# A transformer block on one core: silu, sums of squares and a third of the first modulation columns moved to TensorE's row and column groups

## The chip, the cores and the metric

One core of a Trainium2 chip runs the whole program. The metric is device microseconds of one execution; before the change the median of three runs is 1647.77 us (1646.96 to 1654.14).

## The reference, cut to what matters

The block has 256 tokens of width 2048. What matters here is its beginning:

```python
mod = silu(c) @ w_ada + b_ada                 # c: 2048, w_ada: 2048 x 12288
sh1, sc1, gt1, sh2, sc2, gt2 = split(mod, 6)
h = rms_norm(x, norm1_g) * (1.0 + sc1) + sh1  # x: 256 x 2048
proj = h @ w_in                               # w_in: 2048 x 10064
```

Behind it come a recurrent mix (RWKV-7), a sparse attention, a merge, an output projection and a feed-forward part of width 8192. All is fp32 to the outside; the change touches nothing behind proj.

## The kernel before, in words

x and h stand transposed, 16 chunks of 128 model columns by 256 tokens. Each weight is split on the chip into a high part, rounded by ScalarE (`whi`, line 193), and a low part, the difference, by VectorE (`wlo`, line 90); h likewise (`hhi`, `hlo`). A product is three matmuls (`mm3`): high by high, high by low, low by high.

**The modulation.** Column e of mod (128 values) is a dot product of 128 rows of w_ada transposed with silu(c), which stands on every partition (`sb`). `ada_long` (line 164) loads one such tile of 128x2048 (1 MB) into a slot of `ap0` or `ap1` on the SP queue, and VectorE multiplies and sums it in one operation (line 158), which gives one column of `modc`. Four slots are used for the first four loads, afterwards two (`SLOTS`).

**silu(c).** c arrives as one row of 2048; four fp32 matmuls with a row of ones spread it over the partitions (`cps`), ScalarE takes a tanh, VectorE forms twice the silu in `sb`.

**The squares.** ScalarE squares x in eight pieces of two chunks, VectorE adds them up (`sqs`, seven additions), and two matmuls with ones sum over the partitions (`pss`); `rsqrt` makes the factor `rs` of it.

**The rounds.** h is needed chunk by chunk, and chunk j needs columns j (shift) and 16 + j (scale). So the first projections run in five rounds over chunks 0-1, 2-3, 4-7, 8-11 and 12-15 (`rounds`). In each round `modulate` (line 325) forms am, hf, hhi and hlo of its chunks; then nine groups of columns of w_in are multiplied with them: one of 352 columns, eight of 512. `proj` (line 244) takes a group; for each pair of chunks it loads a weight tile (`weights`, 512 KB, four `raw` buffers, three each of whi and wlo) and lets `next_ada` load columns of the next round at an even pace (`pace`). From the second round on VectorE adds a group's PSUM to what stands in SBUF; the two groups of v stay in PSUM. Of two pairs a group has two weight tiles, so the second round has 9 tiles and the third and fourth 18.

The order of the work is set by priorities (`prio`: START first, then STREAM for weights, MAIN for matmuls) and a scheduler that simulates a timeline and writes each engine's instructions in one fixed order. Each engine, and the SP queue that issues these loads, then works strictly in that order.

Of the kernel before, what the change touches and what calls it, by code (L numbers as in the profile page):

```python
# [11 lines left out]
FT = mybir.dt.float32  # L12
# [5 lines left out]
T = 256  # L18
# [5 lines left out]


P_BADA, P_N1, P_N2, P_MU, P_A0, P_KK, P_KA, P_RK, P_LNW, P_LNB = 0, 96, 112, 128, 155, 163, 171, 179, 187, 195
P_QG, P_KG0, P_KG1, P_KG2, P_PEK, P_PEV, NPRM = 203, 204, 205, 206, 207, 223, 239

C_ID, C_MSK, C_HS, C_ONE, C_BLK, C_CUM, C_SEL, NCST = 0, 128, 192, 224, 225, 353, 609, 737

# [2 lines left out]
def block_kernel(ctx, tc, a):  # L33
# [32 lines left out]
    def B8(name, shape, dt=FT):  # L66
        return b8.tile(shape, dt, name=name, tag="b8")
# [4 lines left out]
    def T2(name, shape, dt=FT):  # L72
        return t2.tile(shape, dt, name=name, tag="t2")
# [7 lines left out]
    def PM(name, shape=(128, 512)):  # L81
        return pmm.tile(list(shape), FT, name=name, tag="pm")
# [3 lines left out]
    def act(out, in_, func, **kw):  # L86
        return S.activation(out, in_, func, **kw).ins  # L87

    def tt(out, x, y, op):
        return V.tensor_tensor(out, x, y, op=op).ins  # L90
# [7 lines left out]
    def mm(out, l, r, start=True, stop=True):  # L98
        return PE.matmul(out, l, r, start=start, stop=stop, skip_group_check=True).ins  # L99
# [10 lines left out]

    tc.cur_priority = START
    sb = sbp.tile([128, D], FT, name="sb", tag="sb")
    crow = B8("crow", [1, D])
    nc.sync.dma_start(crow, a["c"])
    one1 = cst.tile([1, 128], FT, name="one1")
    V.memset(one1, 1.0)
    xn = B16("xn", [128, KC, T])
    xT = a["xT"].rearrange("(k p) t -> p k t", p=128)
# [21 lines left out]
    ts(qg8, prm[:, P_QG:P_QG + 1], 0.125, None, OP.mult, OP.bypass)  # L140


    for i in range(4):
        ps = PM("cps")
        mm(ps, one1, crow[:, i * 512:i * 512 + 512])
        o = sb[:, i * 512:i * 512 + 512]
        lastt = act(o, ps, AF.Tanh, scale=0.5)
        stt(o, o, 1.0, ps, OP.add, OP.mult)
# [11 lines left out]

    apb = [B16("ap0", [128, 2, D]), B16("ap1", [128, 2, D])]
    apn = [0]
    SLOTS = 2

    def ada_long(e):

        n = apn[0] if apn[0] < 4 else apn[0] % SLOTS
        r = apb[n // 2][:, n % 2]
        apn[0] += 1
        nc.sync.dma_start(r, a["w_ada_t"][e * 128:(e + 1) * 128])  # L170
        ada_dot(r, sb, prm[:, P_BADA + e:P_BADA + e + 1], modc[:, e:e + 1])

    def ada(e):

        part = sm.tile([128, 1], FT, name="adap", tag="sm1")
        for h in range(2):
            r = RAW("ar", [128, 1024])
            nc.sync.dma_start(r, a["w_ada_t"][e * 128:(e + 1) * 128, h * 1024:(h + 1) * 1024])
            ada_dot(r, sb[:, h * 1024:(h + 1) * 1024], part if h else prm[:, P_BADA + e:P_BADA + e + 1],
                    modc[:, e:e + 1] if h else part)  # L180

    rounds = [(0, 2), (2, 2), (4, 4), (8, 4), (12, 4)]
    for j in range(rounds[0][1]):
# [52 lines left out]
    def next_ada(f=ada):  # L236
        pace[1] += pace[0]
        while later and pace[1] >= 1:
            pace[1] -= 1
            with prio(STREAM):  # L240
                f(later.pop(0))

    def proj(segs_of, W, ms, rhi, rlo, kps, evac, banks=None, first=True, last=True):


        nb = (len(ms) + 1) // 2
        ps = banks or [PM("pp") for _ in range(nb)]
        for i, kp in enumerate(kps):
            hi, lo = weights(segs_of(kp), W)
            next_ada(ada_long if starting[0] else ada)  # L250
            todo = [[(k, m) for m in range(len(ms))] for k in range(2)]
            if 0 and i == len(kps) - 1 and nb == 2:
                todo = [[(k, m) for k in range(2) for m in range(len(ms)) if m // 2 == b] for b in range(2)]
            for part in todo:
                for k, m in part:
                    (c0, cw), kc = ms[m], 2 * kp + k
                    o = ps[m // 2][0:cw, (m % 2) * 256:(m % 2) * 256 + 256]
                    mm3(o, hi[:, k, c0:c0 + cw], lo[:, k, c0:c0 + cw], rhi[:, kc], rlo[:, kc],
                        first and i == 0 and k == 0 and m % 2 == 0, last and i == len(kps) - 1 and k == 1)
                yield  # L260
        if evac:
            with prio(STREAM):
                for b in range(nb):
                    evac(b, ps[b])
# [17 lines left out]


    pss = PX("pss", (128, 256))
    sqs = T2("sqs", [128, 2, T])
    act(sqs, xn[:, 0:2], AF.Square)
    for i in range(1, 8):
        sq = T2("sq", [128, 2, T])
        act(sq, xn[:, 2 * i:2 * i + 2], AF.Square)
        tt(sqs, sqs, sq, OP.add)  # L290
    for k in range(2):
        mm(pss, ones, sqs[:, k], k == 0, k == 1)

    def log_exp(behind):

# [5 lines left out]
    def rsqrt(out, x, scale, ep, tmp):  # L301

        e0 = {0.0: 0, 1e-6: 1, 64e-5: 2}[ep]
        act(out, x, AF.Ln, scale=scale, bias=eps[0:x.shape[0], e0:e0 + 1])
        i = act(out, out, AF.Exp, scale=-0.5)
        tt(tmp, out, out, OP.mult)
        stt(tmp, x, ep / scale, tmp, OP.add, OP.mult)
        stt(tmp, tmp, -0.5 * scale, out, OP.mult, OP.mult)
        stt(out, out, 1.5, tmp, OP.mult, OP.add)
        return i  # L310

    rs = T2("rs", [128, T])
    with tc.issue_after(log_exp([lastt])):
        rsqrt(rs, pss, 1.0 / D, 1e-6, T2("rst", [128, T]))

    hhi = B16("hhi", [128, KC, T], FR)
    hlo = B16("hlo", [128, KC, T], FR)
# [8 lines left out]
    def modulate(j0, n, src):  # L326

        last = [None]
        for j in range(j0, j0 + n, 2):
            hf = T2("hf", [128, 2, T])  # L330
            for i in range(2):
                affine(hf[:, i], src[:, j + i], am[:, j + i:j + i + 1], rs, modc[:, j + i:j + i + 1], hhi[:, j + i], hlo[:, j + i], last)
        return last[0]

# [49 lines left out]
    for r, (j0, n) in enumerate(rounds):  # L384
        first, last = r == 0, r == len(rounds) - 1
        with prio(START + (1 << 18)):
            stt(am[:, j0:j0 + n], modc[:, 16 + j0:16 + j0 + n], 1.0, prm[:, P_N1 + j0:P_N1 + j0 + n], OP.add, OP.mult)
            lasth = modulate(j0, n, xn)
            if first:
                hold.extend([lasth] * 0 + [None])  # L390
        if not last:
            later.extend(e for j in range(j0 + n, sum(rounds[r + 1])) for e in (j, 16 + j))
            pace[:] = [len(later) / (len(groups) * n // 2 - 1), 0]
        for cols, W, ms, dst, banks in groups:
            g = proj(wseg(cols), W, ms, hhi, hlo, range(j0 // 2, (j0 + n) // 2),
                     dst and acc_evac(dst, first, last), banks, first or banks is None, last or banks is None)
            if last and dst and cols[0][0] >= 3360 and W == 512:
                queue.append(g)
            else:
                run(g)  # L400
        assert not later
    starting[0] = False
    pace[:] = [0.36, 0]

# [728 lines left out]
            lastss[0] = mm(ps[:, 0:T], ones, x[:, i], k == 0 and i == 0, k == 1 and i == 1)  # L1133
    rs2 = T2("rs2", [128, T])
    with tc.issue_after(le):
        i = rsqrt(rs2, ps[:, 0:T], 1.0 / D, 1e-6, T2("rst2", [128, T]))
    ahold[:0] = [i, i]
    for q, t in ((0, 0), (0, 1), (1, 0)):
        tokens(q, t)
# [113 lines left out]
def _pack(inp):  # L1253

    g = {k: v[0] if k != "rel_bias" else v for k, v in inp.items()}
    p = np.zeros((128, NPRM), np.float32)

    def cols(at, v):
        v = v.reshape(-1, 128)
        p[:, at:at + v.shape[0]] = v.T  # L1260

    cols(P_BADA, g["b_ada"])
    cols(P_N1, g["norm1_g"])
    cols(P_N2, g["norm2_g"])
    cols(P_MU, g["rwkv_mu"][:3328])
    p[64:96, P_MU + 26] = g["rwkv_mu"][3328:]
    for at, k in ((P_A0, "rwkv_a0"), (P_KK, "rwkv_k_k"), (P_KA, "rwkv_k_a"), (P_LNW, "rwkv_ln_w"), (P_LNB, "rwkv_ln_b")):
        cols(at, g[k])
    cols(P_RK, g["rwkv_r_k"].reshape(-1))
    for at, v in ((P_QG, g["q_norm_g"]), (P_KG0, g["k_norm_g"][0]), (P_KG1, g["k_norm_g"][1]), (P_KG2, g["k_norm_g"][2])):  # L1270
        p[:, at] = np.concatenate([v, v])
    for at, k in ((P_PEK, "cmp_pe_k"), (P_PEV, "cmp_pe_v")):
        p[:, at:at + 16] = g[k].reshape(16, 2, 64).transpose(1, 2, 0).reshape(128, 16)
    c, onehot = _consts()
    out = {
        "xT": g["x"].T, "c": g["c"], "w_ada_t": g["w_ada"].T, "w_in": g["w_in"], "params": p, "consts": c,
        "onehot": onehot, "w2a": np.concatenate([g["rwkv_w2"], g["rwkv_w0"][None]]), "a2": g["rwkv_a2"],
        "g2": g["rwkv_g2"], "w1k": g["cmp_w1_k"], "w2k": g["cmp_w2_k"], "w1v": g["cmp_w1_v"], "w2v": g["cmp_w2_v"],
        "rel_bias": g["rel_bias"], "w_o_rwkv": g["w_o_rwkv"], "w_o_nsa": g["w_o_nsa"], "w_out": g["w_out"],
        "w_up": g["w_up"], "w_down": g["w_down"],  # L1280
    }
    return {k: np.ascontiguousarray(v) for k, v in out.items()}
# [17 lines left out]
```

## Time and profile before

| | |
|---|---|
| runs: median, lowest, highest | 1647.77, 1646.96, 1654.14 us |
| profiled execution: its time | 1648.3 us |
| its span, first to last instruction | 1646.5 us |
| mean granted TensorE clock | 0.983 |
| TensorE, VectorE, ScalarE busy | 95%, 70%, 46% |

The profile is of one execution. Its busy figures are means over stages that differ much, so a stage is read by its own windows. Engine names are PE (TensorE matmul), PEld (its weight loads), DVE (VectorE), ACT (ScalarE), SPq (the queue that issues loads). Ends of matmuls are modelled, so a matmul is shown longer than the distance to the next one.

### The profile page before, as it was taken

How to read it: one execution, taken by the hardware profiler on the slowest of the kernel's cores; microseconds unless marked ns; L12 is line 12 of the kernel's file. 1: busy time of each engine (PE TensorE's matmuls, PEld its weight loads, DVE VectorE, ACT ScalarE, POOL GpSimd, SP SyncE). 2: the span in 40 equal slices, each digit the busy share in tenths (PEclk: the TensorE clock that was granted, in tenths of full speed). 3: DMA queues.
4: the chain of work that ended last, by engine and by line, in shares of the span. 5: the costliest groups of instructions: out<-in, count | busy, mean ns of one | idle time of the engine just before them, and what ended most of it. 6: DMA issues, size and time to landing. Idle time of an engine off the chain costs nothing.

```text
span 1646.5 us, 28130 instructions
## 1 busy us (share of the span) xinstructions
PE 1564.2 (95%) x11291; PEld 1380.2 (84%) x11291; DVE 1149.4 (70%) x1695; ACT 756.3 (46%) x1112; POOL 34.9 (2%) x60
## 2 busy tenths in 40 slices
PE   5969999999999889999999899999999999999998
PEld 4968998878889879777899788888888888888886
DVE  7999876977788766777876776666655555555555
ACT  4423358526423365656534444444444544444442
POOL 0000000000000000000000000000000000000001
PEclk9989999998999999999999999999999999999999
DMA  9999767673988777655687477878776555555564
GB/s 371 319 325 342 247 183 236 215 200 120 324 245 276 251 262 258 237 180 167 212 287 269 153 242 239 264 244 260 242 217 189 204 194 193 192 192 194 194 194 148
DMA packets 171174, 381.99 MB, mean 232 GB/s; under 512 B 29249, under 2 KB 43905, under 8 KB 166690
## 3 DMA queue, kind: packets, MB, share of 16 engines
q1 hardware_dynamic: 149344, 355.79, 65.6%
q0 software_dynamic: 4176, 14.17, 2.4%
q10 hardware_dynamic: 17523, 10.24, 2.2%
q8 instruction: 88, 1.44, 0.3%
q14 instruction: 43, 0.35, 0.1%
HBM read 370.13 MB, written 10.01 MB: 231 GB/s over the span
## 4 chain that ended last, share of the span: by engine, by line
PE 48%; DMA 4%; DVE 3%; issue 1%; ACT 1%; DVEq 0%; ACTq 0%
PE pu L99 21%; PE da L99 10%; PE db L99 10%; PE pp L99 5%; DMA ar<-in_w_ada_t 2%; DMA wr<-in_w_out 1%; DVE wlo L90 1%; PE po L99 1%; PE sps L99 1%; DMA gate<-sma 0%; ACT whi L193 0%; PE ptp L1012 0%; DVE ar L158 0%; DVE o L90 0%; ACT p L87 0%
## 5 line engine op out<-in xcount | busy, mean ns | idle before, releaser
L193 ACT CAST whi<-wr 128x1024 fp32r<-128x1024 f32 (+1 forms) x352 | 367.0, 1043 | 513.4 <-PE pp L99 125.6
L90 DVE TENSOR_TENSOR wlo<-wr,whi 128x1024 fp32r<-128x1024 f32 (+1 forms) x352 | 425.8, 1213 | 171.8 <-ACT whi L193 168.7
L99 PE MATMUL pp<-hhi,whi 128*128 128x256 f32 (+1 forms) x1072 | 309.9, 293 | 25.1 <-ACT hhi L87 22.5
L99 PE MATMUL pp<-hlo,whi 128*128 128x256 f32 (+1 forms) x1072 | 307.4, 289 | 0.2 <-DVE hlo L93 0.2
L99 PE MATMUL pp<-hhi,wlo 128*128 128x256 f32 (+1 forms) x1072 | 301.2, 290 | 6.6 <-DVE wlo L90 6.6
L90 DVE TENSOR_TENSOR wdl<-wd,wdh 128x1024 fp32r<-128x1024 f32 x128 | 156.6, 1225 | 170.9 <-ACT wdh L193 170.9
L99 PEld LDWEIGHTS pp<-hhi,whi 128*128 128x128 f32 (+1 forms) x1072 | 209.9, 197 | 33.8 <-ACT hhi L87 23.4
L193 ACT CAST wdh<-wd 128x1024 fp32r<-128x1024 f32 x128 | 134.9, 1055 | 193.7 <-PE db L99 188.6
L99 PEld LDWEIGHTS pp<-hhi,wlo 128*128 128x128 f32 (+1 forms) x1072 | 205.5, 196 | 13.0 <-DVE wlo L90 8.5
L99 PEld LDWEIGHTS pp<-hlo,whi 128*128 128x128 f32 (+1 forms) x1072 | 210.5, 196 | 5.0 <-issue 3.7
L99 PE MATMUL pu<-h2a,whi 128*128 128x512 f32 x512 | 177.2, 398 | 3.1 <-DVE h2a L93 3.1
L99 PE MATMUL pu<-h2b,whi 128*128 128x512 f32 x512 | 179.1, 397 | 0.8 <-DVE h2b L93 0.8
L99 PE MATMUL pu<-h2b,wlo 128*128 128x256 f32 x512 | 140.9, 280 | 0.0
L99 PE MATMUL pu<-h2a,wlo 128*128 128x256 f32 x512 | 135.9, 281 | 0.0
L158 DVE CUSTOM_DVE_ANT_0 ar<-ar,sb,prm 128x1024 f32<-128x1024 f32 x64 | 82.1, 1282 | 73.0 <-DMA ar<-in_w_ada_t 72.9
L99 PEld LDWEIGHTS pu<-h2b,whi 128*128 128x128 f32 x512 | 95.8, 188 | 23.9 <-DVE h2b L93 1.2
L99 PEld LDWEIGHTS pu<-h2a,whi 128*128 128x128 f32 x512 | 95.2, 189 | 24.4 <-DVE h2a L93 3.4
L99 PEld LDWEIGHTS pu<-h2a,wlo 128*128 128x128 f32 x512 | 95.5, 190 | 2.2
L158 DVE CUSTOM_DVE_ANT_0 ar<-ar,sb,adap 128x1024 f32<-128x1024 f32 x64 | 82.0, 1281 | 21.2 <-DMA ar<-in_w_ada_t 20.9
L99 PEld LDWEIGHTS pu<-h2b,wlo 128*128 128x128 f32 x512 | 95.9, 189 | 0.5
L99 PE MATMUL db<-wdh,ul 128*128 128x512 f32 x256 | 79.6, 389 | 0.0
L99 PE MATMUL db<-wdl,uh 128*128 128x512 f32 x256 | 79.6, 389 | 0.0
(342 smaller groups left out, 2676.6 us busy)
## 6 DMA issues: line engine op xcount, KB each, us to landing
wr<-in_w_in SPq DMA_DIRECT2D x136, 512.0 KB, 5.1
ar<-in_w_ada_t SPq DMA_DIRECT2D x128, 512.0 KB, 4.8
wr<-in_w_up SPq DMA_DIRECT2D x128, 512.0 KB, 4.3
wd<-in_w_down SPq DMA_DIRECT2D x128, 512.0 KB, 4.3
ap<-in_w_ada_t SPq DMA_DIRECT2D x32, 1024.0 KB, 6.6
wr<-in_w_out SPq DMA_DIRECT2D x32, 512.0 KB, 5.4
wr<-in_w_in SPq DMA_DIRECT2D x40, 256.0 KB, 3.4
wr<-in_w_o_rwkv SPq DMA_DIRECT2D x16, 512.0 KB, 4.9
```

The lines of the kernel that those rows point to most:

```text
L90: return V.tensor_tensor(out, x, y, op=op).ins
L99: return PE.matmul(out, l, r, start=start, stop=stop, skip_group_check=True).ins
L158: V.tensor_tensor_reduce(out=r, in0=r, in1=s, scale=0.5, scalar=start, op0=OP.mult, op1=OP.add, accum_out=out)
L193: S.copy(hi, raw)
```

## The change

Five edits:

1. c is loaded as four rows of 512 on partitions 0, 32, 64 and 96, and the four spreading matmuls take one row each, into four PSUM banks, ahead of the tanhs.
2. The squares of x go to TensorE: each piece's two halves are summed over the partitions into one of four column groups of `ps4` (16 matmuls of 32 columns), copied, and one matmul with ones sums the groups. The additions on VectorE go.
3. In the first round h is formed one chunk at a time, in later ones two.
4. `ada_long` always uses four slots.
5. For the third, fourth and fifth rounds half of the eight modulation columns come from TensorE. Of the four chunks the first two keep their four dot products. The columns of the other two are loaded as four tiles of a repacked array `w_ada_p`, 128x2048 each (`ada_rows`). Once all four are loaded, and at least three weight tiles after the last was issued, `rows_done` issues 16 fp32 matmuls with silu(c) as a weight of 32 columns, one of them not zero (`scz`), into four column groups of one PSUM bank; ScalarE copies the bank; four matmuls of one column turn the sums into four columns; two small VectorE operations add the bias. The pace is set so that the last load comes earlier in the round.

```diff
 P_QG, ..., NPRM = 203, 204, 205, 206, 207, 223, 239
...
-    crow = B8("crow", [1, D])
-    nc.sync.dma_start(crow, a["c"])
-    one1 = cst.tile([1, 128], FT, name="one1")
+    crow = T2("crow", [128, 512])
+    nc.sync.dma_start(crow.rearrange("(g r) n -> g r n", g=4)[:, 0], a["c"].rearrange("(g n) -> g n", g=4))
+    one1 = cst.tile([128, 128], FT, name="one1")
...
+    cps = [PM("cps") for _ in range(4)]
     for i in range(4):
-        ps = PM("cps")
-        mm(ps, one1, crow[:, i * 512:i * 512 + 512])
+        mm(cps[i], one1[32 * i:32 * i + 1], crow[32 * i:32 * i + 1])
+    for i, ps in enumerate(cps):
         o = sb[:, i * 512:i * 512 + 512]
...
-        n = apn[0] if apn[0] < 4 else apn[0] % SLOTS
+        n = apn[0] % 4
...
+    scz = T2("scz", [128, 16, 32])
+    V.memset(scz, 0.0)
+    sct = T2("sct", [128, 16])
+    act(sct, prm[:, P_C:P_C + 16], AF.Tanh, scale=0.5)
+    stt(scz[:, :, 0], sct, 1.0, prm[:, P_C:P_C + 16], OP.add, OP.mult)
+    loaded = []
+
+    def ada_rows(x):
+        j, q = x
+        r = apb[apn[0] % 4 // 2][:, apn[0] % 2]
+        apn[0] += 1
+        nc.sync.dma_start(r, a["w_ada_p"][(j - 6 + q) * 128:(j - 5 + q) * 128])
+        loaded.append([j, r, 0])
+
+    def rows_done(all_of_them=False):
+
+        for x in loaded:
+            x[2] += 1
+        if len(loaded) < 4 or loaded[-1][2] < 3 and not all_of_them:
+            return
+        ps = PM("adp")
+        for q in range(4):
+            for i in range(4):
+                mm(ps[32 * i:32 * i + 32], scz[:, 4 * q + i], loaded[q][1][:, i * 512:i * 512 + 512], q == 0, q == 3)
+        j = loaded[0][0]
+        del loaded[:4]
+        row = T2("adr", [128, 512])
+        S.copy(row, ps)
+        for i in range(4):
+            mm(ps[:, i:i + 1], row[:, i * 128:i * 128 + 128], one, i == 0, i == 3)
+        for i, e in enumerate((j, 16 + j)):
+            stt(modc[:, e:e + 2], ps[:, 2 * i:2 * i + 2], 0.5, prm[:, P_BADA + e:P_BADA + e + 2], OP.mult, OP.add)
...
-            next_ada(ada_long if starting[0] else ada)
+            next_ada((ada_rows if later and isinstance(later[0], tuple) else ada_long) if starting[0] else ada)
...
+                if starting[0] and part is todo[1]:
+                    rows_done()
                 yield
...
-    sqs = T2("sqs", [128, 2, T])
-    act(sqs, xn[:, 0:2], AF.Square)
-    for i in range(1, 8):
+    ps4 = PX("ps4", (128, 256))
+    for i in range(8):
         sq = T2("sq", [128, 2, T])
         act(sq, xn[:, 2 * i:2 * i + 2], AF.Square)
-        tt(sqs, sqs, sq, OP.add)
-    for k in range(2):
-        mm(pss, ones, sqs[:, k], k == 0, k == 1)
+        for k in range(2):
+            g = 2 * (i % 2) + k
+            mm(ps4[32 * g:32 * g + 32], ones[:, 0:32], sq[:, k], i < 2, i > 5)
+    sq4 = T2("sq4", [128, T])
+    S.copy(sq4, ps4)
+    mm(pss, ones, sq4)
...
-            stt(am[:, j0:j0 + n], modc[:, 16 + j0:16 + j0 + n], 1.0, prm[:, P_N1 + j0:P_N1 + j0 + n], OP.add, OP.mult)
-            lasth = modulate(j0, n, xn)
+            step = 1 if first else 2
+            for j in range(j0, j0 + n, step):
+                stt(am[:, j:j + step], modc[:, 16 + j:16 + j + step], 1.0, prm[:, P_N1 + j:P_N1 + j + step], OP.add, OP.mult)
+                lasth = modulate(j, step, xn)
...
             pace[:] = [len(later) / (len(groups) * n // 2 - 1), 0]
+            if r:
+                j = j0 + n
+
+                later[:] = [j, 16 + j, j + 1, 17 + j] + [(j + 2, q) for q in range(4)]
+                pace[:] = [8 / (len(groups) * n // 2 - 4), 0]
...
         assert not later
+        rows_done(True)
     starting[0] = False
```

Left out are small parts: c as 16 more columns of the parameters (`P_C`), the factor 32 that the row of ones of `ps4` brings into `rsqrt`'s scale, a return value of `rsqrt`, and the packing of `w_ada_p` outside the device program.

## Rows read from the trace of the kernel before

**Rows 1.** The page: its span, TensorE's total, TensorE in 40 slices.

```profile
span 1646.5 us, 28130 instructions
...
PE 1564.2 (95%) x11291; PEld 1380.2 (84%) x11291; DVE 1149.4 (70%) x1695; ACT 756.3 (46%) x1112; POOL 34.9 (2%) x60
...
PE   5969999999999889999999899999999999999998
```

**Rows 2.** Ten-us windows: busy time of each engine (x instructions), PEclk, DMA share, GB/s.

```profile
0.00:10.00 10.00, 7.05 (x8) 2.49 (x8) 4.90 (x17) 6.11 (x11) 0.20 (x4) 1.00 0.82 283
10.00:20.00 10.00, 2.19 (x5) 1.18 (x4) 9.12 (x11) 4.39 (x8) 0.00 (x0) 1.00 1.00 418
20.00:30.00 10.00, 1.94 (x7) 1.65 (x8) 9.97 (x17) 3.78 (x5) 0.00 (x0) 1.00 1.05 411
30.00:40.00 10.00, 10.00 (x76) 10.00 (x75) 6.75 (x7) 5.41 (x9) 0.00 (x0) 1.00 1.03 389
...
70.00:80.00 10.00, 10.00 (x86) 10.00 (x85) 10.00 (x10) 2.89 (x3) 0.00 (x0) 1.00 0.98 333
```

**Rows 3.** Windows, TensorE alone: busy time (x matmuls), PEclk, DMA share, GB/s.

```profile
83.00:95.20 12.20, 0.00 (x0) 0.67 0.94 326
95.20:103.00 7.80, 7.63 (x43) 0.64 0.73 262
108.00:163.00 55.00, 50.26 (x400) 0.97 0.97 345
163.00:208.00 45.00, 45.00 (x378) 1.00 0.76 251
```

**Rows 4.** TensorE's waits, 80 to 110 us and 140 to 160 us.

```profile
PE pp L99 <- ACT hhi L87: 13.4, 1, 13.4
...
PE pp L99 <- DVE wlo L90: 3.7, 3, 2.2
```

**Rows 5.** VectorE's timeline: last dot of round two, x scaled behind it.

```profile
91.70 2.35 DVE L158 CUSTOM_DVE_ANT_0 ap<-ap,sb,prm 128x2048 f32<-128x2048 f32 x1 [1.33 <-DMA ap<-in_w_ada_t]
...
94.29 1.67 DVE L93 SCALAR_TENSOR_TENSOR hf<-xn,am,rs 128x256 f32<-128x256 f32 x4
```

**Rows 6.** VectorE's groups, 95 to 206 us: low parts, dot products.

```profile
L90 DVE TENSOR_TENSOR wlo<-wr,whi 128x1024 fp32r<-128x1024 f32 (+1 forms) x35 | 40.8, 1181 | 6.8 <-ACT whi L193 6.8
L158 DVE CUSTOM_DVE_ANT_0 ap<-ap,sb,prm 128x2048 f32<-128x2048 f32 x16 | 37.5, 2345 | 3.0 <-DMA ap<-in_w_ada_t 3.0
```

**Rows 7.** Loads to 260 us: count, KB each, median us to landing.

```profile
wr<-in_w_in SPq DMA_DIRECT2D x68, 512.0 KB, 5.5
ap<-in_w_ada_t SPq DMA_DIRECT2D x32, 1024.0 KB, 6.6
```

**Rows 8.** The SP queue's own waits to 260 us: us, times, longest.

```profile
SPq L170 <- DVE modc L158: 57.2, 24, 5.3
```

**Rows 9.** TensorE's timeline: fp32 matmuls of 32 columns by 512.

```profile
281.41 0.28 PE L99 MATMUL pp<-hlo,whi 128*128 128x256 f32 x1
281.62 1.04 PE L99 MATMUL kss<-ksq,cs 128*32 128x512 f32 x2
...
288.02 1.05 PE L99 MATMUL kss<-ksq,cs 128*32 128x512 f32 x4
```

**Rows 10.** TensorE's timeline: fp32 transposes with 128x128 weights, two places.

```profile
379.81 0.60 PE L638 MATMUL vps<-cs,pv 128*128 128x128 f32 x4
380.17 0.36 PE L99 MATMUL pp<-hhi,whi 128*128 128x256 f32 x1
...
398.28 1.97 PE L660 MATMUL bkp<-cs,BK 128*128 128x128 f32 x8
```

**Rows 11.** ScalarE's groups, 28 to 206 us: the copies of a PSUM bank.

```profile
L359 ACT COPY prk<-pp 128x512 f32<-128x512 f32 x8 | 4.6, 589 | 3.6 <-PE pp L99 3.6
```

**Rows 12.** ScalarE's timeline at the start: first weight's cast, first h.

```profile
21.20 0.78 ACT L193 CAST whi<-wr 128x704 fp32r<-128x704 f32 x1 [1.44 <-DMA wr<-in_w_in]
...
27.33 0.91 ACT L87 ACTIVATE hhi<-hf,modc 128x256 fp32r<-128x256 f32 x2 [2.56 <-DVE hf L93]
```

**Rows 13.** VectorE's groups to 28 us: the additions of squares.

```profile
L90 DVE TENSOR_TENSOR sqs<-sqs,sq 128x512 f32<-128x512 f32 x7 | 4.8, 690 | 1.4 <-ACT sq L87 1.1
```

More of the change, by code (lines that the diff above doesn't have):

```diff
@@ L26 @@
 P_BADA, P_N1, P_N2, P_MU, P_A0, P_KK, P_KA, P_RK, P_LNW, P_LNB = 0, 96, 112, 128, 155, 163, 171, 179, 187, 195
-P_QG, P_KG0, P_KG1, P_KG2, P_PEK, P_PEV, NPRM = 203, 204, 205, 206, 207, 223, 239
+P_QG, P_KG0, P_KG1, P_KG2, P_PEK, P_PEV, P_C, NPRM = 203, 204, 205, 206, 207, 223, 239, 255
 C_ID, C_MSK, C_HS, C_ONE, C_BLK, C_CUM, C_SEL, NCST = 0, 128, 192, 224, 225, 353, 609, 737
@@ L162, in block_kernel @@
     apn = [0]
-    SLOTS = 2
     def ada_long(e):
-        n = apn[0] if apn[0] < 4 else apn[0] % SLOTS
+        n = apn[0] % 4
         r = apb[n // 2][:, n % 2]
@@ L308, in rsqrt @@
         stt(tmp, tmp, -0.5 * scale, out, OP.mult, OP.mult)
-        stt(out, out, 1.5, tmp, OP.mult, OP.add)
-        return i
+        return i, stt(out, out, 1.5, tmp, OP.mult, OP.add)
     rs = T2("rs", [128, T])
     with tc.issue_after(log_exp([lastt])):
-        rsqrt(rs, pss, 1.0 / D, 1e-6, T2("rst", [128, T]))
+        rsqrt(rs, pss, 1.0 / (32 * D), 1e-6, T2("rst", [128, T]))
     hhi = B16("hhi", [128, KC, T], FR)
@@ L330, in modulate @@
             hf = T2("hf", [128, 2, T])
-            for i in range(2):
+            for i in range(min(2, n)):
                 affine(hf[:, i], src[:, j + i], am[:, j + i:j + i + 1], rs, modc[:, j + i:j + i + 1], hhi[:, j + i], hlo[:, j + i], last)
@@ L1135, in block_kernel @@
     with tc.issue_after(le):
-        i = rsqrt(rs2, ps[:, 0:T], 1.0 / D, 1e-6, T2("rst2", [128, T]))
+        i = rsqrt(rs2, ps[:, 0:T], 1.0 / D, 1e-6, T2("rst2", [128, T]))[0]
     ahold[:0] = [i, i]
@@ L1266, in _pack @@
     p[64:96, P_MU + 26] = g["rwkv_mu"][3328:]
+    cols(P_C, g["c"])
     for at, k in ((P_A0, "rwkv_a0"), (P_KK, "rwkv_k_k"), (P_KA, "rwkv_k_a"), (P_LNW, "rwkv_ln_w"), (P_LNB, "rwkv_ln_b")):
@@ L1275, in _pack @@
     out = {
-        "xT": g["x"].T, "c": g["c"], "w_ada_t": g["w_ada"].T, "w_in": g["w_in"], "params": p, "consts": c,
+        "xT": g["x"].T, "c": g["c"], "w_ada_t": g["w_ada"].T,
+        "w_ada_p": np.concatenate([np.concatenate([g["w_ada"][:, e:e + 256] for e in (j * 128, D + j * 128)], 1)
+                                   .reshape(4, 4, 128, 512).transpose(0, 2, 1, 3).reshape(512, D) for j in (6, 10, 14)]),
+        "w_in": g["w_in"], "params": p, "consts": c,
         "onehot": onehot, "w2a": np.concatenate([g["rwkv_w2"], g["rwkv_w0"][None]]), "a2": g["rwkv_a2"],
```

## The prediction

> **What bounds the kernel now.** I read the page first: TensorE is busy 95% of the span, and its two lowest slices of 41 us are the first and the third [rows 1]. So the kernel is bound by TensorE nearly everywhere, an edit is worth the TensorE time it removes or adds, and all that the diff touches lies in the first 208 us. There I read the ten-microsecond windows for the DMA rate [rows 2], then the count of matmuls per stretch [rows 3], TensorE's waits [rows 4], and last the VectorE timeline at the longest wait [rows 5].
>
> What is to be seen: undisturbed, TensorE issues 378 matmuls in 45 us, 0.119 us each [rows 3]; a group's weight tile (24 matmuls) takes 2.86 us, the first one (18) 2.14 us, a pair of chunks 25 us. It falls short in three places. It starts at about 28 us. Between 82 and 95.4 us it stands still for 13.4 us [rows 4] for the third round's h: the second round is one pair of chunks long, and eight dot products of 2.35 us have to be done in it on VectorE, the last from 91.70 to 94.05 us, with the scaling of x behind it [rows 5]. After this pause the granted clock averages 0.64 for 7.8 us, so part of it is at 1.2 GHz: 43 matmuls in place of 66 [rows 3], 2.7 us lost. I count the third round as starting at 98.0 us at full speed. From 108 to 163 us there are 400 matmuls in place of 462 [rows 3], 7.4 us lost, of which the waits that are named are late low parts of weights [rows 4]: VectorE spends 40.8 us on these and 37.5 us on dot products in one stretch [rows 6], about evenly.
>
> **The sum** is made against the profiled execution's 1648.3 us; the median of the runs is 0.5 us less.
>
> *Second round.* The bytes moved stay the same: a row tile is 1024 KB like the column load it replaces [rows 7]. But four slots in place of two let a load be issued before the dot two back is done; that wait cost the SP queue 57.2 us [rows 8], and every weight tile behind it in the queue waited too. Up to the second round's last weight tile 28.5 MB must move (x 2.1, constants 0.5, 16 loads 16.8, two pairs of chunks 9.1; sizes from rows 7, the 352-column tiles from the code). 2.8 MB are moved by 10 us, and the rate from 10 to 40 us is 418, 411, 389 GB/s; later, with short queues, it is 333 [rows 2]. At the mean of the first three, 406, the last tile lands at 73.2 us and the sixth of the nine, the first behind the last row tile in the queue, three tiles or 3.9 us earlier, at 69.4 us. 1.2 us later (its cast) TensorE can take it, and the four tiles from the sixth to the ninth, 2.86 us each, bring the round to 82.0 us, without the new work.
>
> *New TensorE work, per round, three times.* 16 fp32 matmuls of 32 columns by 512. The nearest row is of the same shape: one such matmul (two instructions) shows 1.04 us, and two in neighbouring column groups show 1.05 us together [rows 9]; their streams run beside each other. A matmul's shown time is longer than its place in the queue, 0.28 against 0.119 us for the usual one [rows 3, 9], so one occupies about 1.04 - 0.16 = 0.88 us. If four groups stream in the time of one, it is 4 x 0.88 = 3.5 us, plus some 0.2 at the change of shape. Bounds: 3.5, and 16 x 0.88 = 14.1 us if nothing ran beside anything. I take 3.7, since the row is the same operation. A page speaks against this price: the Trainium skill, TensorE: Matmul & The Clock Gate, Part 3 (measured speedup), has 3.07x for four row tiles and 2.38x for three column tiles, not four and three; by 3.07 the 16 would cost 4.6 us, and the sum below would be about 3 us worse. Rows 9 show no loss at two groups; none shows four. Then four fp32 matmuls of one column (eight instructions with 128x128 weights): behind four transposes with such weights the next matmul starts 0.36 us after the first of them, eight elsewhere take 1.97 [rows 10]; so 0.7 to 2.0, I take 1.1. Together 4.8 us per round.
>
> In the second round these come, in program order, after the seventh tile: 82.0 + 4.8 = 86.8 us. If they are put where TensorE waits for the sixth tile (from 65.8 to 70.6 us, with a start at 24.5, 2.7 us lost to the lower clock as above, 25 us for the first pair and 13.6 for five tiles) they are free: 82.0. I take 86.8. Gain at this point: 98.0 - 86.8 = 11.2 us. The earlier start does not enter, since the transfers set the end of this round.
>
> *Third and fourth round.* Eight dots and their 19 us leave VectorE here, so most of the 7.4 us goes; I leave 1.0: +6.4. Two times 4.8 us is added with TensorE otherwise full: -9.6. The small matmuls wait for ScalarE's copy of the row (0.59 us [rows 11]) and stand in TensorE's queue before weight-tile matmuls: free if other matmuls are put between, up to 1.9 us if a cast of 1.05 is ahead of the copy. 1 us each: -2.0. Behind the row sum come two small operations on VectorE, am, hf and hhi, about 3 us, covered by the last tile of the old round and the first of the new one (5.0 us). If that cover shrank, the next round would start late by the rest. Sum: 11.2 + 6.4 - 9.6 - 2.0 = 6.0 us, and 1648.3 - 6.0 = **1642.3**.
>
> *Costed at nothing.* First h chunk by chunk, silu by row groups and the squares: TensorE could start at 22.0 us, when the first weight tile is cast (21.20 + 0.78), in place of 27.9, when h is there [rows 12]; 4.8 us of VectorE additions go [rows 13] for matmuls on an idle TensorE. I expect a start near 24.5 us, hidden by the transfers. If it were not hidden it would give up to 5.9 us; if c's matmuls did not run side by side, the dot products, which wait for their loads, would begin where they do now. The memsets of one1 and scz fill VectorE's idle first microseconds. The extra tanh and 16 columns of parameters are hidden by x's loads. scz keeps one of seven t2 buffers and the row result one of four PSUM banks; a group needs two banks, so the group after next may wait a few tenths. On the SP queue a row tile waits for its slot's dot (landed 10 us before) and weight tiles wait behind it; since casts are also four tiles ahead, I put nothing.
>
> **Rivals.** *The new work hides and the waits go.* The row matmuls lie in the wait for the sixth tile, the third and fourth rounds have no late small matmul: 16.0 + 6.4 - 9.6 = 12.8 us, 1635.5. For it: the wait is 4.8 us, the work 4.8. Against: program order puts the work two tiles later.
>
> *The transfers stay slow.* If from 40 us on the rate remains the 333 GB/s of 70 to 80 us [rows 2], the sixth tile lands at 75.8 us, the third round starts at 93.2 and the sum is 4.8 - 5.2 = -0.4: 1648.7. For it: the DMA engines were 0.98 busy at that rate. Against: 10 to 30 us show over 410 with the same kinds of load. A page has it this way: the Trainium skill, DMA: Bandwidth & Descriptors, Specifications, gives a limit of about 358 GB/s of HBM for a core; the trace exceeds it [rows 2].
>
> *Slower: the column groups do not run four at a time.* With a price c per round in place of 4.8 the gain is 20.4 - 3c. Two at a time, c = 8.3: 1652.8. One after another, c = 15.4: 1674. It is slower by over 0.5% from c = 9.5. Against: rows 9. For: no row has four.
>
> **Numbers.** 0.5% is 8.2 us, about what a measurement of this kernel tells from no change. The forecast 0.45; hidden 0.33; slow transfers 0.10; groups two by two or one by one, 0.12. The forecast reaches over 8.2 us at its cheap end (c = 4.2, no late copies: 9.8 us), so faster is 0.38; slower takes most of the last case: 0.13; same 0.49. The range runs from the hidden case with part of the earlier start, 1631, to past two at a time, 1654; the serial case stays out.
>
> **What would show it.** Right: the wait for hhi near 82 us is gone or under 4 us; the DMA rate from 40 to 75 us near 400; the first matmul at 22 to 26 us; 16 row matmuls in about 3.7 us; matmuls per 5 us from 108 us on without gaps but for some 5 us per round of row work; about 29 us less VectorE. Wrong: 16 row matmuls over 7 us; a new TensorE wait for the copied row or a row tile; a rate still near 330; or a later stage shifting by more than this sum.

## The result, and the profile after

The changed kernel takes 1669.64 us (median of four runs, 1666.28 to 1673.03) against 1647.37 us for the kernel before on the same chip: ratio 1.0137 (1.0111 to 1.0164). It is slower by some 22 us, where 6 us less were forecast, and it lies outside the range. The profiled execution of after took 1666.28 us, its span is 1664.5, 18.0 above the span in [rows 1].

The page of after, its totals and slices, beside [rows 1]:

```profile
span 1664.5 us, 28430 instructions
...
PE 1584.7 (95%) x11441; PEld 1389.0 (83%) x11441; DVE 1124.1 (68%) x1676; ACT 761.5 (46%) x1117; POOL 35.1 (2%) x60
...
PE   5889899999999979999999899999999999999998
```

The totals alone would not tell a loss: VectorE has 25 us less, TensorE the same share. So the rounds are read one by one. A mark that every kernel has is VectorE's first addition to `pl` in a round, which is the end of the round's first group; the last mark is the first `zps` matmul, the work behind the rounds. The times below are starts in us, read from the timelines of VectorE and TensorE.

| | round 2 | round 3 | round 4 | round 5 | behind the rounds | span |
|---|---|---|---|---|---|---|
| before | 57.5 | 104.5 | 159.9 | 210.5 | 249.7 | 1646.5 |
| after | 61.6 | 114.7 | 182.0 | 237.4 | 272.3 | 1664.5 |
| after is later by | 4.1 | 10.2 | 22.1 | 26.9 | 22.6 | 18.0 |

Each boundary loses some: 4.1, 6.1, 11.8 and 4.8 us, and the last stretch gives 4.3 back. Behind the rounds the gap shrinks by another 4.6 us, in code that the change does not touch; that is taken up last.

Every mark is read from one execution. How far executions part can be seen where kernels run the same instructions in the same order: after, e3 and e12 (below) do so up to their first row matmul, which starts at 85.49, 85.06 and 83.45 us. So a difference of some 2 us between two marks tells nothing.

**What came as forecast.** The new TensorE work, in TensorE's timeline of after (start, busy us, operation):

```profile
2.95 2.09 PE L99 MATMUL cps<-crow,one 1*128 1x512 f32 x8 [2.95 <-DMA crow<-in_c]
...
85.49 3.64 PE L99 MATMUL adp<-ap,scz 128*32 128x512 f32 x32
89.06 0.39 PE L99 MATMUL pp<-hhi,whi 128*128 128x256 f32 x1
...
92.16 0.95 PE L99 MATMUL adp<-cs,adr 128*128 128x1 f32 x8
```

The 16 row matmuls (two instructions each) hold TensorE for 89.06 - 85.49 = 3.57 us; four column groups do stream side by side. The column matmuls take 0.95. The same four matmuls of c that took 7.16 us before take 2.09. The transfers run at the forecast rate too, in windows of after against [rows 2]:

```profile
10.00:70.00 60.00, 42.18 (x296) 1.00 1.03 404
```

404 GB/s over the 60 us from 10 to 70 us, against the 406 of the sum.

**What did not.** The order of the SP queue's loads, its timeline first in before, then in after:

```profile
43.39 0.34 SPq L170 DMA_DIRECT2D ap<-in_w_ada_t  x1
44.53 0.37 SPq L226 DMA_DIRECT2D wr<-in_w_in  x1
46.80 0.34 SPq L170 DMA_DIRECT2D ap<-in_w_ada_t  x1
49.16 3.29 SPq L226 DMA_DIRECT2D wr<-in_w_in  x3
55.15 0.34 SPq L170 DMA_DIRECT2D ap<-in_w_ada_t  x1
56.29 0.37 SPq L226 DMA_DIRECT2D wr<-in_w_in  x1
```

```profile
42.13 7.32 SPq L262 DMA_DIRECT2D wr<-in_w_in  x5
49.55 2.03 SPq L196 DMA_DIRECT2D ap<-in_w_ada_p  x2
53.30 0.38 SPq L262 DMA_DIRECT2D wr<-in_w_in  x1
54.71 1.83 SPq L196 DMA_DIRECT2D ap<-in_w_ada_p  x2
57.58 27.73 SPq L262 DMA_DIRECT2D wr<-in_w_in  x14
```

In before the modulation loads of this stretch go out one at a time, with weights between. In after all four row tiles are issued by 56.5 us, with the next 14 loads of weights behind them. Counted over the whole timeline, before has issued 19 loads of w_in and 11 of the modulation by 57 us, after 16 and 16. In the 20 us from 40 to 60 TensorE gets 129 matmuls in after and 169 in before (TensorE's windows, first before, then after):

```profile
40.00:60.00 20.00, 20.00 (x169) 1.00 0.93 318
```

```profile
40.00:60.00 20.00, 16.45 (x129) 1.00 1.03 405
```

The engine that was full is now waiting, while the transfers run faster than before: what moves is not what TensorE needs next. Forty matmuls of 0.119 us are the 4.8 us of which the mark of round 2 shows 4.1. At 69 to 71 us it happens again, in ScalarE's and TensorE's timelines of after and in a window of TensorE:

```profile
70.43 1.04 ACT L229 CAST whi<-wr 128x1024 fp32r<-128x1024 f32 x1 [5.38 <-DMA wr<-in_w_in]
...
71.53 0.38 PE L99 MATMUL pvp<-hhi,whi 128*128 128x256 f32 x1 [2.16 <-ACT whi L229]
...
71.50:76.00 4.50, 3.95 (x21) 0.70 0.62 174
```

ScalarE waits 5.38 us for the weight tile that is first behind the row tiles, TensorE 2.16 us for ScalarE, and behind the wait (last line, TensorE's window from 71.5 us) the granted clock averages 0.70, so part of that stretch is at 1.2 GHz.

The other loss stands at the boundaries. VectorE's timeline of after, at the start of the third round:

```profile
97.15 0.22 DVE L93 SCALAR_TENSOR_TENSOR modc<-adp,prm 128x2 f32<-128x2 f32 x2
97.29 0.68 DVE L90 TENSOR_TENSOR pq<-pq,pp 128x512 f32<-128x512 f32 x1
97.88 2.34 DVE L160 CUSTOM_DVE_ANT_0 ap<-ap,sb,prm 128x2048 f32<-128x2048 f32 x1
...
100.15 0.15 DVE L93 SCALAR_TENSOR_TENSOR am<-modc,prm 128x2 f32<-128x2 f32 x1
...
101.96 2.35 DVE L160 CUSTOM_DVE_ANT_0 ap<-ap,sb,prm 128x2048 f32<-128x2048 f32 x1
...
104.23 0.88 DVE L93 SCALAR_TENSOR_TENSOR hf<-xn,am,rs 128x256 f32<-128x256 f32 x2
...
106.16 2.35 DVE L160 CUSTOM_DVE_ANT_0 ap<-ap,sb,prm 128x2048 f32<-128x2048 f32 x1
...
108.43 0.88 DVE L93 SCALAR_TENSOR_TENSOR hlo<-hf,modc,hhi 128x256 fp32r<-128x256 f32 x2
```

From the row sum's columns (97.15) to the h made of them (109.31) go 12.2 us; three dots of the next round, 7.0 us, stand between. They are there because row tiles hold all four slots until the row matmuls at 85.5 us: the next round's four column loads can only be issued then (86.62 to 89.5 us on the SP queue). They land one behind another up to 101.9 us, and their dots come just when h is due. TensorE's timeline of after shows who pays, at this boundary and at the next:

```profile
105.30 0.74 PE L99 MATMUL pp<-hhi,whi 128*128 128x256 f32 x4 [0.56 <-ACT hhi L87]
108.96 0.58 PE L99 MATMUL pp<-hlo,whi 128*128 128x256 f32 x1 [2.92 <-DVE hlo L93]
...
172.76 1.22 PE L99 MATMUL pp<-hhi,whi 128*128 128x256 f32 x4 [4.04 <-ACT hhi L87]
176.42 0.58 PE L99 MATMUL pp<-hlo,whi 128*128 128x256 f32 x1 [2.44 <-DVE hlo L93]
```

Two such stretches in TensorE's windows of after, with some shorter waits in them:

```profile
98.00:110.00 12.00, 6.90 (x48) 0.89 1.02 406
164.00:177.00 13.00, 6.09 (x40) 0.82 1.02 412
```

48 and 40 matmuls stand where 101 and 109 would fit at 0.119 us: 6.3 and 8.2 us gone. The granted clock averages 0.89 and 0.82, so part of each stretch is at 1.2 GHz.

### The profile page after: what moved, and what is told of

Same layout as the page of the kernel before. It is cut to its first block, busy times and chain, and to the rows that moved or that the text cites. A ratio compares the mean times of both kernels' runs of the same rounds, so it can differ in the third digit from the quotient of the medians.

```text
span 1664.5 us, 28430 instructions
## 1 busy us (share of the span) xinstructions
PE 1584.7 (95%) x11441; PEld 1389.0 (83%) x11441; DVE 1124.1 (68%) x1676; ACT 761.5 (46%) x1117; POOL 35.1 (2%) x60
## 4 chain that ended last, share of the span: by engine, by line
PE 74%; DMA 11%; DVE 9%; issue 3%; ACT 2%; ACTq 0%; SPq 0%; DVEq 0%
PE pp L99 22%; PE pu L99 21%; PE da L99 10%; PE db L99 10%; DMA ar<-in_w_ada_t 3%; DVE wlo L90 3%; DMA wr<-in_w_in 3%; PE pvp L99 2%; DMA wr<-in_w_out 2%; DVE ap L160 2%; PE po L99 1%; PE sps L99 1%; ACT whi L229 1%; DVE ar L160 1%; DMA kx<-skv 1%
## 5 line engine op out<-in xcount | busy, mean ns | idle before, releaser
L99 PE MATMUL pp<-hhi,whi 128*128 128x256 f32 (+1 forms) x1072 | 310.0, 294 | 19.2 <-ACT hhi L87 14.5
L99 PEld LDWEIGHTS pp<-hlo,whi 128*128 128x128 f32 (+1 forms) x1072 | 209.6, 196 | 11.3 <-DVE hlo L93 8.2
L99 PEld LDWEIGHTS pu<-h2a,whi 128*128 128x128 f32 x512 | 95.1, 189 | 24.5 <-DVE h2a L93 3.5
```

## The experiments

Three causes are to be told apart: the row work itself (theory C in the expectations); the order of the SP queue (theory B); the place of the dots on VectorE (theory A). Behind the second and third stands one edit, the four slots that dots and row tiles share. Twelve kernels were run; their marks, as in the table above, stand together here (times in us; the ratio to the kernel before on the same chip). The runs were made on several chips, so medians are compared by their ratios.

| | median | ratio | round 2 | round 3 | round 4 | round 5 | behind the rounds |
|---|---|---|---|---|---|---|---|
| e1 no row tiles | 1664.82 | 1.0096 (1.0058 to 1.0133) | 64.3 | 110.9 | 173.2 | 223.5 | 262.7 |
| e2 before, four slots | 1672.82 | 1.0147 (1.0118 to 1.0177) | 65.7 | 111.8 | 174.2 | 224.5 | 263.7 |
| e3 dots behind h | 1654.40 | 1.0048 (1.0033 to 1.0063) | 61.3 | 105.7 | 167.5 | 222.9 | 257.8 |
| e4 weights first on SP | 1659.88 | 1.0074 (1.0049 to 1.0100) | 57.8 | 106.8 | 170.8 | 225.9 | 260.8 |
| e5 both | 1659.18 | 1.0084 (1.0053 to 1.0116) | 56.3 | 101.2 | 160.9 | 217.5 | 252.4 |
| e6 start alone, two slots | 1644.97 | 0.9999 (0.9981 to 1.0018) | 56.6 | 103.3 | 157.5 | 206.0 | 245.1 |
| e7 e5, row sum earlier | 1669.91 | 1.0147 (1.0116 to 1.0177) | 56.9 | 100.2 | 155.7 | 209.6 | 248.7 |
| e8 e2, weights first | 1660.96 | 1.0089 (1.0056 to 1.0122) | 58.8 | 102.4 | 162.0 | 212.4 | 249.6 |
| e9 own buffers | 1651.53 | 1.0016 (0.9997 to 1.0036) | 57.8 | 99.3 | 161.8 | 216.8 | 251.7 |
| e10 e9, dots behind h | 1658.92 | 1.0063 (1.0043 to 1.0084) | 58.1 | 97.6 | 163.0 | 220.3 | 255.3 |
| e11 e9, third round only | 1650.63 | 1.0014 (0.9994 to 1.0035) | 58.5 | 103.2 | 158.9 | 207.5 | 246.7 |
| e12 e3, a quarter of the row work | 1649.64 | 1.0002 (0.9978 to 1.0025) | 62.6 | 101.9 | 162.1 | 215.3 | 250.2 |

The last column is the measure of the rounds; the medians also hold what the stage behind does (below). An added order constraint can also make the scheduler place other instructions anew, so an edit is not always the only difference between two kernels.

**e1: after without the row tiles**; all columns are dots again, with four slots.

```diff
-            if r:
-                j = j0 + n
-                later[:] = [j, 16 + j, j + 1, 17 + j] + [(j + 2, q) for q in range(4)]
-                pace[:] = [8 / (len(groups) * n // 2 - 4), 0]
```

> The changed kernel with all modulation columns as dot products on VectorE again; the other edits stay (silu and squares on TensorE's groups, first h by chunks, four slots). Theory A (VectorE runs the next round's four dot products ahead of the scaling of the last two chunks at two round boundaries, because the row tiles hold all slots until then): the two stalls of 8 to 11 us and the three lots of 4.6 us of row work on TensorE are gone, 1640 to 1648 us. Theory B (four slots let loads run ahead of weight tiles and starve TensorE in the second round): still over 1655 us. Theory C (only the TensorE work itself, 14 us): about 1653 us.

The rounds end at 262.7 us, 9.6 before after but still 13.0 behind before. So the row work alone is not what makes the change slow: with none of it, more than half of the loss stands, and the time is where theory B had it (over 1655 us).

**e2: before with four slots**, one number changed.

```diff
-    SLOTS = 2
+    SLOTS = 4
```

> The kernel before with four slots in place of two and nothing else. Theory B: slower than before by 5 us or more, with waits of TensorE for weights between 50 and 75 us. Theories A and C: no slower than before; the wait for the third round's h (13.4 us) shrinks, as the prediction had it, 1635 to 1648 us.

This line alone costs 14.0 us at the end of the rounds, as theory B expected (the rest of the 1.0147 arises behind them). TensorE's waits from 28 to 260 us in e2 and its window of 40 to 60 us show where:

```profile
PE pp L99 <- DVE wlo L90: 13.2, 8, 2.5
PE pp L99 <- ACT hhi L87: 9.1, 1, 9.1
PE pvp L99 <- DVE wlo L90: 5.5, 3, 3.3
PE pp L99 <- ACT whi L193: 3.2, 2, 1.6
...
40.00:60.00 20.00, 15.36 (x120) 1.00 1.03 416
```

Weights are late: 120 matmuls against 169, with the transfers at 416 GB/s in place of 318. The wait of 9.1 us for `hhi` is the one before the first matmul, which the kernel before has too. Its wait of 13.4 us for the third round's h [rows 4] does not occur in e2: what the prediction expected of the slots is there, and late weights cost more than it gives.

**e3: after with the dots behind h** on VectorE, from the third round on. `issue_after` is a constraint on the program's scheduler: the dots may not be placed ahead of the round's last h instruction.

```diff
+            if r > 1:
+                modl[0] = lasth
...
-        ada_dot(r, sb, prm[:, P_BADA + e:P_BADA + e + 1], modc[:, e:e + 1])
+        with tc.issue_after(modl[0]) if modl[0] else contextlib.nullcontext():
+            ada_dot(r, sb, prm[:, P_BADA + e:P_BADA + e + 1], modc[:, e:e + 1])
```

> The changed kernel, but from the third round on VectorE takes a round's dot products only behind the last scaling of that round's h. Theory A: the waits for h's high and low part near 105 and 173 us go, 15 to 19 us back, 1648 to 1655 us. Theories B and C: no change, 1664 to 1672 us.

The rounds end 14.5 us earlier and the ratio falls from 1.0137 to 1.0048 (1654.40 us, inside theory A's range). VectorE's timeline of e3 at the same boundary, against after's:

```profile
93.35 0.22 DVE L93 SCALAR_TENSOR_TENSOR modc<-adp,prm 128x2 f32<-128x2 f32 x2
93.60 0.16 DVE L93 SCALAR_TENSOR_TENSOR am<-modc,prm 128x2 f32<-128x2 f32 x1
93.80 0.88 DVE L93 SCALAR_TENSOR_TENSOR hf<-xn,am,rs 128x256 f32<-128x256 f32 x2
...
96.19 0.48 DVE L93 SCALAR_TENSOR_TENSOR hlo<-hf,modc,hhi 128x256 fp32r<-128x256 f32 x1
96.58 2.35 DVE L160 CUSTOM_DVE_ANT_0 ap<-ap,sb,prm 128x2048 f32<-128x2048 f32 x1
```

The chain from the row sum to h takes 3.3 us (93.35 to 96.67) in place of 12.2. The mark of round 2 stays at 61.3: the first loss is another one.

**e4: after with the weights first on the SP queue**; each modulation load is placed behind the last weight load before it in the program.

```diff
-        nc.sync.dma_start(r, a["w_ada_p"][(j - 6 + q) * 128:(j - 5 + q) * 128])
+        with tc.issue_after(lastw[0]):
+            nc.sync.dma_start(r, a["w_ada_p"][(j - 6 + q) * 128:(j - 5 + q) * 128])
```

(and the same in `ada_long`; `lastw` is set in `weights`.)

> The changed kernel, but each modulation load is issued on the SP queue behind the weight tile that stands before it in the program. Theory B: in the second round weights no longer land behind all row tiles (the fourth tile was the first behind them, not the sixth), TensorE reaches the third round 5 to 6 us earlier, 1660 to 1665 us. Theory A: the boundaries' stalls stay, so no more than that, or nothing.

Now the window from 40 to 60 us is full again (the window of e4), the mark of round 2 is back at 57.8, and the rounds end 11.5 us earlier, more than the 5 to 6 us of theory B:

```profile
40.00:60.00 20.00, 20.00 (x169) 1.00 1.02 389
```

**e5: both orders**, the edits of e3 and e4 together.

> Both orders at once: dot products behind the round's h on VectorE, and each modulation load behind its weight tile on the SP queue. If theories A and B are two separate losses, they add: 1667 less 12 to 15 less 6 to 9 us, 1643 to 1650 us, and the first matmul behind the rounds comes at 245 to 252 us (changed kernel: 272.3; before: 249.7). If they are one loss seen twice, no better than the dot order alone, 1652 to 1657 us.

The two gains add for the most part: 19.9 us of the 26.0 that they had alone, of the 22.6 to be explained. The 2.7 us that are left are little more than two executions can part by. So the two orders account for the loss in the rounds. The total misses the expectation: the ratio falls to 1.0084 only (1659.18 us, 1643 to 1650 expected), because the stage behind the rounds takes 680.3 us here against 670.9 in after.

**e6: the start's edits alone**, with two slots and no row tiles.

```diff
-        n = apn[0] % 4
+        n = apn[0] if apn[0] < 4 else apn[0] % 2
```

(and e1's edit.)

> The kernel before with the start alone (c by row groups, squares by column groups, h chunk by chunk), two slots and no row tiles. Theory B (four slots do the harm): no slower than before, 1638 to 1648 us. If the start edits do harm by themselves (their chunks' order, the scheduler's new order behind them): 1652 us or more.

The rounds end 4.6 us before those of the kernel before; in the time of the whole this is not to be told from no change. Beside e1 it is a second test of the slots: the programs of e1 and e6 differ by the number of slots alone, and by 17.6 us at the end of the rounds.

**e7: e5 with the row sum earlier**, one weight tile behind the last row tile in place of three.

```diff
-        if len(loaded) < 4 or loaded[-1][2] < 3 and not all_of_them:
+        if len(loaded) < 4 or loaded[-1][2] < 1 and not all_of_them:
```

> As both orders, and the row matmuls are issued one weight tile after the last row tile was issued, not three. If what is left is that the row tiles hold all four slots too long, so that the next round's loads come late: 3 to 6 us under both orders alone. If TensorE then waits for row tiles that have not landed: slower than it.

The rounds end 3.7 us earlier than e5's, as expected, yet the kernel is 10.7 us slower. All of that arises behind the rounds (below).

**e8: e2 with the weights first**, e4's constraint on the kernel before with four slots.

> The kernel before with four slots, each modulation load behind its weight tile on the SP queue. Theory B (four slots harm because loads run ahead of weight tiles): the 25 us that four slots cost go, and with the longer queue it is no slower than before, 1640 to 1650 us. If four slots harm through VectorE's order (dot products taken earlier than h and low parts), it stays over 1660 us.

The rounds end at 249.6 us, where the kernel before ends them (249.7), against 263.7 in e2. So with four slots and no row tiles the order of the SP queue is the whole cost of the slots in the rounds. The total, 1660.96 us, is not what was expected and lies where the expectation put the other cause, VectorE's order (over 1660). The marks speak against that cause in the rounds: what is left in the ratio arises behind them, where the stage takes 688.7 us against 676.5.

**e9: after with buffers of their own for the row tiles.** The dots have two slots, as in the kernel before; the row tiles lie in the other two and in two more.

```diff
-        n = apn[0] % 4
+        n = apn[0] if apn[0] < 4 else apn[0] % 2
...
+    rowb = [apb[1][:, 0], apb[1][:, 1]] + [B8("rw", [128, D]) for _ in range(2)]
...
-        r = apb[apn[0] % 4 // 2][:, apn[0] % 2]
-        apn[0] += 1
+        r = rowb[q]
```

> The changed kernel with buffers of their own for the row tiles (the last two slots and two 8 KB buffers that are free in this phase); dot products have the first two slots, as in the kernel before. Theory A, read as a matter of slots: the next round's loads and dots need no longer wait for the row matmuls, and with two slots no load runs far ahead of weight tiles, so both losses go: the first matmul behind the rounds at 240 to 250 us (changed: 272.3; before: 249.7), since the waits of before (about 23 us) go and 14 us of row work come. In all 1638 to 1650 us. If the row tiles' loads alone starve the weights: 255 us or later.

With no order imposed, the rounds end 20.6 us earlier than in after (251.7 us, 240 to 250 expected), and the ratio falls to 1.0016, which is not to be told from the kernel before. TensorE's waits from 28 to 260 us, first after, then e9:

```profile
PE pp L99 <- DVE hlo L93: 7.2, 4, 2.9
PE pp L99 <- ACT hhi L87: 4.6, 2, 4.0
PE pp L99 <- DVE wlo L90: 2.6, 4, 0.9
```

```profile
PE pp L99 <- DVE wlo L90: 6.2, 5, 2.9
...
PE pp L99 <- ACT hhi L87: 0.4, 1, 0.4
...
PE pp L99 <- DVE hlo L93: 0.2, 1, 0.2
```

The waits for h are gone; those for low parts grow. In the second round the row matmuls start at 76.75 us in place of 85.49. One of the next round's dots is done before the row sum's columns (87.32 us); a second still stands between these and the h made of them, which takes 8.5 us here, but TensorE does not get there sooner. e9 changes two things at once, the row tiles' buffers and the dots' slots (two again, as in the kernel before), and no run has one without the other; so the 20.6 us belong to both together.

**e10: e9 with e3's edit.**

> As with own buffers, and dot products behind the round's h. If own buffers already remove the clump at the boundary, no further change at the first matmul behind the rounds (within 3 us); if the order on VectorE is a loss of its own, 4 to 10 us earlier.

It does not help: the third round is 1.7 us earlier, the end of the rounds 3.6 us later. That is neither of the two expected outcomes. e9 has no wait for h left that the order could remove; what makes e10 later was not traced.

**e11: e9 with row tiles for the third round alone.**

```diff
-            if r:
+            if r == 1:
```

> As with own buffers, but only the third round's columns come from TensorE; the fourth and fifth round's are dot products. By the prediction's sum the row work (4.7 us a round) costs more than the waits it removes in the later two rounds (7.4 us in both): 2 to 5 us better than with own buffers, 1635 to 1646 us. If the later rounds' dots are what fills VectorE and makes weights late: slower than with own buffers.

The rounds end at 246.7 us, between e6 (none, 245.1) and e9 (three rounds, 251.7): 1.6 us for one round's row work, which two executions can part by, and 6.6 for three, less than the TensorE time of the row work, since dots and waits go in return. The total, 1650.63 us, is not to be told from e9's; 1635 to 1646 was expected. The third round's mark is 103.2, no better than without row tiles, although e9 and e11 run the same instructions up to some 97 us. There e11 is already 1.5 us later, so the 4.0 us that e9 has at this mark cannot be put down to the row tiles.

**e12: e3 with a quarter of the row matmuls' columns.** Of the 16 matmuls 12 have 2 columns in place of 512; half of the later chunks' modulation is therefore not the reference's.

```diff
-                mm(ps[32 * i:32 * i + 32], scz[:, 4 * q + i], loaded[q][1][:, i * 512:i * 512 + 512], q == 0, q == 3)
+                w = 512 if q == 3 else 2
+                mm(ps[32 * i:32 * i + 32, 0:w], scz[:, 4 * q + i], loaded[q][1][:, i * 512:i * 512 + w])
```

> The kernel with dot products behind h, with 512 columns only for the last row tile's four matmuls and 2 columns for the other twelve, so the modulation of half the chunks is not the reference's. Theory C (TensorE's row work lies on the path): three times about 2.6 us less, the first matmul behind the rounds at 249 to 252 us against 257.8. If the work lay in waits, no change.

The rounds end 7.6 us before e3's, as theory C expected. The row matmuls hold TensorE for 1.19 us in place of 3.57, three times, which is 7.1 us. But 1.6 us of the 7.6 stand before the first row matmul already (83.45 against 85.06 us), which leaves 6.0 behind it. So the price of the row work at this place is its TensorE time, as far as single executions tell.

**The stage behind the rounds.** From the first `zps` matmul to the first `pu` matmul no line differs in effect, and the matmuls are the same (one more or less lies at a window's edge). TensorE's windows over this stage, in before, after and e7:

```profile
249.70:926.20 676.50, 640.17 (x6055) 0.97 0.71 230
```

```profile
272.30:943.20 670.90, 640.20 (x6055) 0.97 0.72 232
```

```profile
248.70:950.50 701.80, 652.62 (x6054) 0.95 0.69 222
```

The stage takes 676.5, 670.9 and 701.8 us. The traces say why it can differ at all: of the 9657 matmul instructions from `zps` to the end, 1921 stand at another place of TensorE's order in after than in before, and 2773 in e7. The scheduler plans the whole program, and a change in the rounds re-sorts what follows. But the order is not all. In e9 and e11 only 64 and 60 instructions stand elsewhere than in before, and the stage takes 678.3 and 682.2 us; so after's 5.6 us less are not shown to come from its order.

The 25 us of e7 are more than that, and its four runs lie within 2.3 us. TensorE is busy for 12 us more with the same matmuls, at a mean granted clock of 0.95 in place of 0.97; the rest are waits. The longest new one is 5.1 us for `dh`, which names a symptom. What in e7's order costs the 25 us was not settled, and no run fixes the order behind the rounds.

## Why the prediction was wrong, point by point

- **The step that failed first is in "Costed at nothing":** "On the SP queue ... since casts are also four tiles ahead, I put nothing", and with it the use of the four slots in "Second round" as a gain alone. The wait of the loads for their slots [rows 8] was read as a cost to be removed. It was what kept modulation loads behind the weights. Freed, they go first, the weights come late, and TensorE, full from 40 to 60 us before, has 40 matmuls less there. e2 shows the price of the slots alone, 14.0 us where nothing was put; e8 takes it back to nothing in the rounds, and e4 returns 11.5 of after's 22.6.
- **"The sixth of the nine, the first behind the last row tile"** was the fourth: the row tiles were issued by 56.5 us. Its landing is near the forecast 69.4 us (the cast that waits for it starts at 70.43), but two more tiles, 5.7 us, had to follow it. The end of the round is best read by count, since TensorE takes its last matmuls and the next round's first ones partly in turns. From the fourth tile's start at 71.53 us the six tiles that are left, 144 matmuls, are done at 97.43 us, 10.6 us after the 86.8 of the forecast. The kernel before stands at an equivalent of 98.0 there, so 0.6 of the 11.2 us arrived. Beside the 5.7 us, the tile started 0.9 us later than forecast (70.6), 2.4 us went from 71.5 to 80 us to the lower clock and a wait for a low part (51 matmuls in place of 71), and 1.4 us to a wait for VectorE's addition to `pq`: together 10.4.
- **The cover of 5.0 us in "Third and fourth round"** was the second failed step. The chain from the row sum to h was sized right, 3 us (3.3 in e3), on a VectorE with nothing else to do. That the row tiles keep every slot, so that the next round's dots arrive together just then, was not seen; the chain took 12.2 us. The text had the condition ("if that cover shrank") and no price; e3 puts it at 14.5 us for all the boundaries.
- **The row work was right:** 3.57 + 0.95 = 4.5 us against 4.8, measured in the timeline, and e12 fits it. The rival that the column groups do not run four at a time falls. The page that spoke against the price (the Trainium skill, TensorE: Matmul & The Clock Gate, Part 3: 3.07x for four row tiles, 2.38x for three column tiles) is not borne out here for the column groups: by 3.07 the prediction's estimate for the 16 was 4.6 us, and they took 3.57.
- **The transfers were right:** 404 GB/s against 406, so the rival of slow transfers falls too. The limit of about 358 GB/s for a core (the Trainium skill, DMA: Bandwidth & Descriptors, Specifications) was exceeded for 60 us on end by this one core. After that the rate falls to 223 and 196 GB/s (70 to 90 us), while the row tiles hold all the modulation's slots: its next load is issued at 86.62 us.
- **The start:** the first matmul came at 26.75 us against the 24.5 expected and 27.9 before, and no gain of it is left at the mark of round 2. e6 has it too (26.74), and its rounds end 4.6 us earlier, which the step did not count.
- **VectorE's relief** was near what was said: 25 us less on the page against 29. Without the damage of the shared slots the sum can be read from e9: the third round's mark is 5.2 us earlier, and from there to the end of the rounds 7.2 us are lost, where 11.2 and 5.2 were forecast. The second term was near; of the first, e11, with the same row tiles for the third round, has 1.3 us at this mark, so how much of the 11.2 the change can give stays open.
- **The rival on the slow side** was the wrong one. It priced the new work, whose nearest rows were at hand, and not the resource that the change shares out anew.

## What to carry to other kernels

A wait on a buffer can be an order: before adding buffers to a stream of loads, ask which loads of the same queue would be let past, and who needs the bytes that then come second. Where two uses share a ring of buffers and one of them holds all of it until a sum, the other use arrives in a clump behind that sum; look at what is due on the engine at that moment, or give each use its own buffers (here, with the dots back on two slots, 20.6 us). And with a scheduler that plans the whole program, judge an edit by a mark right behind its stage as well as by the total: the stage that nobody touched took up to 25 us longer.

## What was not expected of the hardware

Four column groups of 32 columns ran 16 fp32 matmuls of 512 columns in 3.57 us, where a lone one shows 1.04 us [rows 9]. By the prediction's estimate of 0.88 us for each, 14.1 us one after another, next to nothing was lost to running four at a time. Four row groups of one row took 2.09 us against 7.16 for the same matmuls one after another, a factor of 3.4. The transfers held 404 GB/s over 60 us, and a faster rate went with a slower TensorE: 405 GB/s with 129 matmuls against 318 with 169.
